# A macaron decoder trunk on one core: five instead of four down-projection units in a seven-product form, and one constant matrix instead of two

## The chip, the core and the metric

The kernel runs on one core of a Trainium2 chip. The metric is the device time of one execution in microseconds (us), as the median of several runs.

## What is computed

A trunk of two residual layers on an input of 256 tokens by 1024 features, in float32. Each layer is a feed-forward network (FFN), a token mixer, and a second FFN; a final RMSNorm follows. So there are four FFNs in the program.

```python
def swiglu(h, w_gate, w_up, w_down):
    return (jax.nn.silu(h @ w_gate) * (h @ w_up)) @ w_down
...
    for layer in range(DEPTH):
        x = x + 0.5 * swiglu(rmsnorm(x, norm_ffn1[layer]), ffn1_gate[layer], ffn1_up[layer], ffn1_down[layer])
        h = rmsnorm(x, norm_mix[layer])
        ...
        x = x + 0.5 * swiglu(rmsnorm(x, norm_ffn2[layer]), ffn2_gate[layer], ffn2_up[layer], ffn2_down[layer])
    return rmsnorm(x, norm_final)
```

What is left out between the two FFNs adds the mixer's output to `x`: stick-breaking attention with pooling in layer 0, block attention in layer 1. The hidden width of an FFN is 2816. Its down projection multiplies the hidden activations (256 tokens by 2816) by a weight matrix of 2816 by 1024.

## The kernel before

**Three passes for one product.** Every float32 operand is split into a high part (a cast to the matmul's rounded float32) and a low part (the operand minus its high part). A product takes three matmuls: high by high, high by low, low by high (`passes`, line 371). For weights, ACT makes the high part (`whi`, line 106) and DVE the low part (`wlo`, line 107), on tiles of 128 partitions by 2048 values.

**The weight stream** (`WeightStream`, lines 38 to 126) loads weights in the order of a list, 1 MB at a time, into 3 raw buffers, and splits them into 4 pairs of `whi` and `wlo` buffers. One entry of the list that is split is called a slot here. `ahead(i)` issues the splits up to three slots ahead; a slot can be split only when the matmuls of the slot four before it are done with its buffers.

**The down projection.** The 2816 hidden rows are 11 units of 256 rows (`r` from 0 to 10). A unit is computed in one of two ways:

- *plain*: 2 row tiles by 2 token halves by 2 column halves by 3 passes, 24 matmuls of 512 columns; the weights are one slot of 2048 values per partition.
- *seven* (Strassen's form): the unit is a 2 by 2 product of blocks, done with 7 block products by 3 passes, 21 matmuls of 512 columns. Its weights take two slots: the *quarters*, for which 1536 of the 2048 raw values are split, and the *sums*: `add_up` (lines 78 to 84) lets DVE make four combinations of the raw quarters with three instructions (lines 82, 83, 84) in the one buffer `sums`, which is then split like raw weights. Three of the seven products use the quarters (9 matmuls), four the sums (12 matmuls).

Below, 5q and 5s are the quarters and the sums of unit 5. `mixed` (lines 424 to 481; its matmuls are recorded at line 444) works off the units of `MIXED`: `SEVEN = [1, 3, 5, 7]`, with plain units 0, 2 and 4 between them. It uses eight PSUM banks, then recombines the products into `x` (lines 469 to 480). `rows` (lines 391 to 422; matmuls at line 413) does the units of `LAST`, all plain, the first of them as one group and the three others as a second, and adds the four accumulators to `x` (line 421).

**The hidden rows** come from the gate and up projections in chunks: chunk `c` makes units `2c-1` and `2c`, in four tiles `f` of 128 rows. `put_pairs` (line 555) follows a chunk: for a unit of the seven form, POOL makes four combinations (lines 564 to 567), ACT casts three pieces into `hs` (line 571) and DVE makes their low parts (line 572); for a plain unit ACT casts one piece into `hp` (line 575) and DVE makes its low part (line 576). In chunk 5 of the kernel before, units 9 and 10 are both plain.

**The order of the work.** Each engine runs its instructions in the order that the framework's scheduler put them in when the program was built, and waits on semaphores for the others. So an instruction that waits holds up all behind it on its engine.

**Room.** `hs` holds the seven-form hidden rows, `hp8` and `hp6` the plain ones; the mixers reuse these three buffers (`mixer_tiles`, line 603). `bcast_rstd` (line 612) turns the norm's factor of each token into a 128-partition row: a diagonal matrix (line 618) times a matrix of ones (line 619).

Of the kernel before, what the change touches and what calls it, by code (L numbers as in the profile page):

```python
# [9 lines left out]
F32 = mybir.dt.float32  # L10
F32R = mybir.dt.float32r
BF16 = mybir.dt.bfloat16
AF = mybir.ActivationFunctionType
ALU = mybir.AluOpType
PSUM = bass.MemoryType.PSUM

P = 128
T = 256
# [9 lines left out]
BIG = 1.0e37  # L28
QK_SCALE = 0.125

SEVEN = [1, 3, 5, 7]
PLAIN = [0, 2, 4, 6, 8, 9, 10]
MIXED = [1, 0, 3, 2, 5, 4, 7]
LAST = [6, 8, 9, 10]
NS = len(SEVEN)


# [114 lines left out]
def trunk_kernel(  # L152
# [6 lines left out]
    nc = tc.nc  # L159
    cp = ctx.enter_context(tc.tile_pool(name="const", bufs=1))  # L160
    wp = ctx.enter_context(tc.tile_pool(name="weights", bufs=1))
    ap_ = ctx.enter_context(tc.tile_pool(name="acts", bufs=1))
# [4 lines left out]
    def uid(s):  # L167
        cnt[0] += 1
        return f"{s}_{cnt[0]}"
# [4 lines left out]
    def tr_bank():  # L174
        return ps.tile([P, 512], F32, tag="tr", name=uid("tr"), bufs=3)

    mm = nc.tensor.matmul
# [6 lines left out]
    def add_cols(key, w, c0):  # L184
        plan[key] = [ws.add(w[0:512, c0 : c0 + 512], 4, 512), ws.add(w[512:1024, c0 : c0 + 512], 4, 512)]
# [4 lines left out]
    def add_rows(key, w, r0, seven=False):  # L190
        plan[key] = ws.add(w[r0 * P : (r0 + 2) * P, :], 2, 1024, seven)

    def add_ffn(tag, wg, wu, wd):
        add_half((tag, "g", 0), wg, 0)
        add_half((tag, "u", 0), wu, 0)
        for c in range(5):
            add_cols((tag, "g", c + 1), wg, 256 + 512 * c)
            add_cols((tag, "u", c + 1), wu, 256 + 512 * c)
        for r in MIXED + LAST:
            add_rows((tag, "d", r), wd, 2 * r, r in SEVEN)  # L200

# [52 lines left out]
    ident = cp.tile([P, P], F32, name="ident")  # L254
    make_identity(nc, ident)
    half = cp.tile([P, 1], F32, name="half")
    nc.gpsimd.memset(half, -0.5)
    ones = cp.tile([P, P], F32, name="ones")
    nc.gpsimd.memset(ones, 1.0)
    gT = [cp.tile([P, n], F32, name=f"gT{n}") for n in (16, 36)]  # L260

    def turn_gains(j):
# [24 lines left out]
    neg1 = cp.tile([P, P], F32, name="neg1")  # L287
# [195 lines left out]
    def first_products(ug, uu):  # L483

        key = ("f1", 0)
        st = states[key]
        with tc.manual_schedule():
            norm_half(0, key, st, ws.split_piece, (1,), True)
            warm_up(3)
            ws.split_to(1)  # L490
            g0 = proj(ug, 0, 256)
            ws.split_to(2)
            norm_half(1, key, st, pool_q=(0, 1))
            u0 = proj(uu, 0, 256)
            ws.split_to(4)
            g1 = proj(ug, 1, 256)
            u1 = proj(uu, 1, 256)
        return [(g0, u0), (g1, u1)]
# [14 lines left out]
    def whole(bank, t):  # L513
        nc.scalar.copy(t, bank[:, T:])  # L514
        nc.vector.tensor_add(t, t, bank[:, :T])  # L515
        return t

    def ffn(tag, st, after, then=lambda: None):
        hs = ap_.tile([P, 2, NS, 7, P], F32R, tag="hs", name=uid("hs"))
        hp = [ap_.tile([P, 2, n, T], F32R, tag=f"hp{n}", name=uid("hp")) for n in (8, 6)]  # L520
        place = {k: j for j, k in enumerate(2 * r + e for r in PLAIN for e in range(2))}

        def plain(k, n=1):

            j = place[k]
            t, j = (hp[0], j) if j < 8 else (hp[1], j - 8)
            return t[:, 0, j : j + n], t[:, 1, j : j + n]

        def put_h(m, h):
            bank = tr_bank()  # L530
            for j in range(2):
                nc.tensor.transpose(bank[:, j * P : (j + 1) * P], h[:, j * P : (j + 1) * P], ident)
            v = bank[:, :T].rearrange("p (k t) -> p k t", k=2)
            hi, lo = (t[:, :, m * P : (m + 1) * P] for t in plain(0, 2))
            nc.scalar.copy(hi, v)
            nc.vector.tensor_sub(lo, v, hi.bitcast(F32))


        ug, uu = plan[tag, "g", 0], plan[tag, "u", 0]
        banks = first_products(ug, uu) if ug[0] == 0 else None  # L540
        ws.ahead(uu[-1])
        for m in range(2):
            g, u = banks[m] if banks else (proj(ug, m, 256), proj(uu, m, 256))
            h = tp.tile([P, T], F32, tag="hw", name=uid("h"), bufs=3)
            nc.scalar.activation(h, g[:, :T], AF.Silu, scale=st[m])
            nc.vector.tensor_mul(h, u[:, :T], h)
            tasks.add(3, lambda m=m, h=h: put_h(m, h))
        box = []
        tasks.add(4, lambda: box.append(bcast_rstd(st)))
        scale = []  # L550
        for m in range(2):
            scale.append(tp.tile([P, 1], F32, tag=f"half_rstd{m}", name=uid("hr")))
            nc.gpsimd.tensor_scalar_mul(scale[m], st[m], 0.5)

        def put_pairs(h, c):

            r = [2 * c - 1, 2 * c]
            n = sum(q in SEVEN for q in r)
            if n:
                v = h.rearrange("p (j e) t -> p j e t", e=2)[:, 0:n]  # L560
                pr = slice(SEVEN.index(r[0]), SEVEN.index(r[0]) + n)
                a11, a21, row2 = v[:, :, 0, 0:P], v[:, :, 0, P:T], v[:, :, 1, :]
                s = tp.tile([P, D], F32, tag="wide", name=uid("s"), bufs=1).rearrange("p (j s t) -> p j s t", j=2, s=4)[:, 0:n]
                nc.gpsimd.tensor_add(s[:, :, 0], a21, row2[:, :, P:T])
                nc.gpsimd.tensor_sub(s[:, :, 2], a21, a11)
                nc.gpsimd.tensor_sub(s[:, :, 1], s[:, :, 0], a11)
                nc.gpsimd.tensor_sub(s[:, :, 3], row2[:, :, 0:P], s[:, :, 1])
                flat = "p j s t -> p j (s t)"
                for d, src in ((slice(0, 1), a11), (slice(1, 3), row2), (slice(3, 7), s.rearrange(flat))):
                    hi, lo = (hs[:, e, pr, d].rearrange(flat) for e in range(2))  # L570
                    nc.scalar.copy(hi, src)
                    nc.vector.tensor_sub(lo, src, hi.bitcast(F32))
            for j in range(n, 2):
                hi, lo = plain(2 * r[j], 2)
                nc.scalar.copy(hi, h[:, 2 * j : 2 * j + 2])  # L575
                nc.vector.tensor_sub(lo, h[:, 2 * j : 2 * j + 2], hi.bitcast(F32))  # L576

        for c in range(1, 6):
            ug, uu = plan[tag, "g", c], plan[tag, "u", c]
            ws.ahead(ug[-1])  # L580
            sg = tp.tile([P, 4, T], F32, tag="sg", name=uid("sg"), bufs=1)
            for f in range(5):
                if f < 4:
                    whole(proj_W(ug, f), sg[:, f])
# [12 lines left out]
        units = [(plan[tag, "d", r], 2 * r, SEVEN.index(r) if r in SEVEN else None) for r in MIXED]
        acc = mixed(units, hs, parts_of, scale)
        then()
        units = [(plan[tag, "d", r], 2 * r) for r in LAST]  # L600
        rows(acc, [units[0:1], units[1:4]], parts_of, scale, after, begun=True)

    def mixer_tiles(n_f):

        o = ap_.tile([P, 2, 8, T], F32R, tag="hp8", name=uid("o"))
        qk = ap_.tile([P, 2 * NS * 7 * P], F32, tag="hs", name=uid("qk"))
        q, k = (qk[:, j * n_f * T : (j + 1) * n_f * T].rearrange("p (f t) -> p f t", t=T) for j in range(2))
        tok = [qk[:, 4096 + j * 1024 : 5120 + j * 1024].rearrange("p (m a) -> p m a", m=2) for j in range(2)]
        room = Room(ap_.tile([P, 2 * 6 * T], F32, tag="hp6", name=uid("room")), qk[:, 6144:])
        return o[:, 0], o[:, 1], q, k, tok, room  # L610

    def bcast_rstd(st):

        bank = tr_bank()
        dg = tp.tile([P, T], F32, tag="hw", name=uid("diag"), bufs=3)
        for m in range(2):
            ms = slice(m * P, (m + 1) * P)
            nc.vector.tensor_scalar_mul(dg[:, ms], ident, st[m])
            mm(bank[:, ms], ones, dg[:, ms], start=True, stop=True)  # L619
        rb = tp.tile([P, T], F32, tag="rb", name=uid("rb"), bufs=1)  # L620
        nc.scalar.copy(rb, bank[:, :T])
        return rb
# [250 lines left out]
```

## Time and profile before

| | us |
|---|---|
| median of 3 runs | 959.95 (959.37 to 959.96) |
| the profiled execution | 959.6 |
| its span, first to last instruction | 957.8 |
| TensorE busy (matmul) | 946.8 |
| VectorE (DVE) busy | 723.3 |
| ScalarE (ACT) busy | 533.5 |
| GpSimd (POOL) busy | 84.3 |

The mean granted clock of TensorE is 0.994 of 2.4 GHz, and half of it in a stretch near the start. A matmul's duration in a row is longer than its pace, since matmuls follow each other in a pipeline: the pace is read from the starts of successive ones. On DVE and ACT too, an instruction starts about 0.1 us before the one ahead of it has ended where nothing has to be waited for.

### The profile page before, as it was taken

To read this page: it belongs to the slowest core of one execution; us is meant where nothing else is said; L and a number is where in the kernel's file an instruction comes from. 1 tells how busy PE (TensorE), PEld (TensorE's weight loads), DVE (VectorE), ACT (ScalarE), POOL (GpSimd) and SP (SyncE) were. 2 spreads that over 40 slices of the span, in tenths; PEclk is the share of its full clock that TensorE was granted. 3 is DMA by queue.
4 is the path that set the end of the run, shared out by engine and by line. 5 is a ranking of instruction groups with operands and counts; after the bars stand their busy time and mean duration, and the time that the engine had idled before them with its cause. 6 is when DMAs were issued, how large, how long until landed. Compare 5 with 4: busy or idle time off the path is not lost.

```text
span 957.8 us, 13148 instructions
## 1 busy us (share of the span) xinstructions
PE 946.8 (99%) x5236; PEld 810.4 (85%) x5236; DVE 723.3 (76%) x953; ACT 533.5 (56%) x749; POOL 84.3 (9%) x158
## 2 busy tenths in 40 slices
PE   8999999999999999999999999999999999999997
PEld 6888888888889888888898888888888798888885
DVE  5777799777656777897767779976887667778974
ACT  6566555466536665555455655536566465665541
POOL 5900000000001000000101000001000010000000
PEclk8999999999999999999999999999999999999998
DMA  7754437654335445546455543764543454445541
GB/s 276 264 177 176 176 137 259 219 177 176 93 128 176 176 176 180 216 176 215 167 208 200 178 176 133 247 233 159 178 150 122 142 177 176 177 176 179 209 161 45
DMA packets 84309, 171.53 MB, mean 179 GB/s; under 512 B 2788, under 2 KB 25880, under 8 KB 84248
## 3 DMA queue, kind: packets, MB, share of 16 engines
q1 hardware_dynamic: 83960, 170.17, 51.1%
q8 instruction: 41, 0.67, 0.3%
q10 hardware_dynamic: 288, 0.52, 0.1%
q14 instruction: 20, 0.16, 0.0%
HBM read 169.63 MB, written 1.05 MB: 178 GB/s over the span
## 4 chain that ended last, share of the span: by engine, by line
PE 98%; DMA 1%; DVE 1%; ACT 0%; issue 0%; SPq 0%; POOLq 0%; POOL 0%; ACTq 0%
PE acc L508 53%; PE acc L413 14%; PE acc L444 11%; PE acc L386 10%; PE tr L444 3%; PE tr L354 1%; PE acc L636 1%; PE tr L746 1%; PE tr L769 1%; DMA raw<-in_ffn_gate_dram 1%; PE tr L659 0%; DVE wlo L107 0%; PE tr L675 0%; PE tr L619 0%; ACT whi L106 0%; PE tr L711 0%
## 5 line engine op out<-in xcount | busy, mean ns | idle before, releaser
L107 DVE TENSOR_TENSOR wlo<-raw,whi 128x2048 fp32r<-128x2048 f32 (+3 forms) x170 | 359.5, 2120 | 98.7 <-ACT whi L106 98.0
L508 PE MATMUL acc<-xhl,whi 128*128 128x512 f32 x1472 | 372.3, 393 | 0.0
L106 ACT CAST whi<-raw 128x2048 fp32r<-128x2048 f32 (+3 forms) x170 | 299.0, 1769 | 92.0 <-PE acc L444 48.6
L508 PEld LDWEIGHTS acc<-xhl,whi 128*128 128x128 f32 x1472 | 264.7, 189 | 47.4 <-issue 0.3
L508 PEld LDWEIGHTS acc<-xhl,wlo 128*128 128x128 f32 x1472 | 200.7, 190 | 15.3 <-issue 1.3
L508 PE MATMUL acc<-xhl,wlo 128*128 128x256 f32 x1472 | 209.8, 283 | 0.0
L386 PE MATMUL acc<-whi,xhl 128*128 128x256 f32 (+1 forms) x416 | 94.3, 316 | 1.1 <-ACT whi L106 1.1
L413 PE MATMUL acc<-whi,hp 128*128 128x512 f32 x256 | 80.6, 392 | 0.0
L386 PEld LDWEIGHTS acc<-whi,xhl 128*128 128x128 f32 x416 | 70.3, 195 | 6.5 <-ACT whi L106 1.8
L386 PE MATMUL acc<-wlo,xhl 128*128 128x256 f32 (+1 forms) x208 | 65.3, 314 | 1.2 <-DVE wlo L107 1.2
L587 ACT ACTIVATE sg<-sg 128x256 f32<-128x256 f32 x80 | 33.0, 417 | 54.3 <-DVE sg L586 54.2
L444 PE MATMUL acc<-whi,hp 128*128 128x512 f32 x192 | 61.1, 389 | 0.0
L514 ACT COPY hw<-acc 128x256 f32<-128x256 f32 x104 | 38.2, 368 | 34.0 <-PE acc L508 33.9
L413 PEld LDWEIGHTS acc<-whi,hp 128*128 128x128 f32 x256 | 47.9, 188 | 9.6
L413 PE MATMUL acc<-wlo,hp 128*128 128x512 f32 x128 | 50.3, 393 | 0.0
L515 DVE TENSOR_TENSOR sg<-sg,acc 128x256 f32<-128x256 f32 x80 | 31.9, 416 | 19.2 <-ACT sg L514 19.1
L515 DVE TENSOR_TENSOR hw<-hw,acc 128x256 f32<-128x256 f32 x104 | 43.1, 414 | 4.2 <-ACT hw L514 4.0
L575 ACT CAST hp<-sg 128x512 fp32r<-128x512 f32 x24 | 14.9, 622 | 54.0 <-DVE sg L591 54.0
L514 ACT COPY sg<-acc 128x256 f32<-128x256 f32 x80 | 27.7, 367 | 31.0 <-DVE hp L576 19.0
L444 PE MATMUL acc<-whi,hs 128*128 128x512 f32 x128 | 44.6, 389 | 0.0
L413 PE MATMUL acc<-whi,o 128*128 128x512 f32 x128 | 43.6, 404 | 0.0
L386 PEld LDWEIGHTS acc<-wlo,xhl 128*128 128x128 f32 x208 | 40.6, 195 | 3.3 <-DVE wlo L107 1.6
(151 smaller groups left out, 1023.2 us busy)
## 6 DMA issues: line engine op xcount, KB each, us to landing
raw<-in_ffn_down_dram SPq DMA_DIRECT2D x44, 1024.0 KB, 4.8
raw<-in_ffn_gate_dram SPq DMA_DIRECT2D x43, 1024.0 KB, 5.0
raw<-in_ffn_up_dram SPq DMA_DIRECT2D x43, 1024.0 KB, 5.0
raw<-in_odd_w_qkv_dram SPq DMA_DIRECT2D x12, 1024.0 KB, 5.0
raw<-in_even_w_in_dram SPq DMA_DIRECT2D x8, 1024.0 KB, 5.6
raw<-in_even_w_out_dram SPq DMA_DIRECT2D x4, 1024.0 KB, 4.7
raw<-in_odd_w_o_dram SPq DMA_DIRECT2D x4, 1024.0 KB, 4.8
raw<-in_ffn_gate_dram SPq DMA_DIRECT2D x2, 512.0 KB, 6.8
```

The lines of the kernel that those rows point to most:

```text
L106: self.nc.scalar.copy(hi[:, d], src)
L107: self.nc.vector.tensor_sub(lo[:, d], src, hi[:, d].bitcast(F32))
L354: nc.tensor.transpose(bank[:, j * P : (j + 1) * P], x[m][:, k * P : (k + 1) * P], ident)
L386: mm(bank[:, :width], a, b, start=(n == 0), stop=(n == len(seq) - 1))
L413: mm(acc[m, n], a, b, start=(done[m, n] == 0 and p == 0 and not begun), stop=(done[m, n] == total - 1 and p == 2), skip_group_check=begun)
L444: mm(b, l, r, start=b.name not in begun, stop=last and n == 2, skip_group_check=True)
L508: mm(dst, w, rhs, start=(n == 0), stop=(n == 2 * KD - 1))
L514: nc.scalar.copy(t, bank[:, T:])
L515: nc.vector.tensor_add(t, t, bank[:, :T])
L575: nc.scalar.copy(hi, h[:, 2 * j : 2 * j + 2])
L587: nc.scalar.activation(sg[:, f - 1], sg[:, f - 1], AF.Silu)
L636: mm(bank[j * HD : (j + 1) * HD, cols], v[:, 0 if start else 1, hs], a[:, s], start=start, stop=not start)
```

## The change

Unit 9 joins the seven form. `MIXED` loses the plain unit 4 and gets unit 9 at its end, so that units 5, 7 and 9 stand in a row, without a plain unit between them; unit 4 becomes the first of `LAST`, before 6, 8 and 10. `hs` grows by a quarter, `hp6` becomes `hp4`, and the mixers' room moves accordingly. The matrix of ones goes: the diagonal is multiplied by -1 in the same instruction, and the matrix of minus ones, which the program has anyway, takes the place of the ones.

```diff
--- before.py
+++ after.py
@@ -28,10 +28,10 @@
 BIG = 1.0e37
 QK_SCALE = 0.125
 
-SEVEN = [1, 3, 5, 7]
-PLAIN = [0, 2, 4, 6, 8, 9, 10]
-MIXED = [1, 0, 3, 2, 5, 4, 7]
-LAST = [6, 8, 9, 10]
+SEVEN = [1, 3, 5, 7, 9]
+PLAIN = [0, 2, 4, 6, 8, 10]
+MIXED = [1, 0, 3, 2, 5, 7, 9]
+LAST = [4, 6, 8, 10]
 NS = len(SEVEN)
 
 
@@ -255,8 +255,6 @@
     make_identity(nc, ident)
     half = cp.tile([P, 1], F32, name="half")
     nc.gpsimd.memset(half, -0.5)
-    ones = cp.tile([P, P], F32, name="ones")
-    nc.gpsimd.memset(ones, 1.0)
     gT = [cp.tile([P, n], F32, name=f"gT{n}") for n in (16, 36)]
 
     def turn_gains(j):
@@ -517,7 +515,7 @@
 
     def ffn(tag, st, after, then=lambda: None):
         hs = ap_.tile([P, 2, NS, 7, P], F32R, tag="hs", name=uid("hs"))
-        hp = [ap_.tile([P, 2, n, T], F32R, tag=f"hp{n}", name=uid("hp")) for n in (8, 6)]
+        hp = [ap_.tile([P, 2, n, T], F32R, tag=f"hp{n}", name=uid("hp")) for n in (8, 4)]
         place = {k: j for j, k in enumerate(2 * r + e for r in PLAIN for e in range(2))}
 
         def plain(k, n=1):
@@ -606,7 +604,7 @@
         qk = ap_.tile([P, 2 * NS * 7 * P], F32, tag="hs", name=uid("qk"))
         q, k = (qk[:, j * n_f * T : (j + 1) * n_f * T].rearrange("p (f t) -> p f t", t=T) for j in range(2))
         tok = [qk[:, 4096 + j * 1024 : 5120 + j * 1024].rearrange("p (m a) -> p m a", m=2) for j in range(2)]
-        room = Room(ap_.tile([P, 2 * 6 * T], F32, tag="hp6", name=uid("room")), qk[:, 6144:])
+        room = Room(ap_.tile([P, 2 * 4 * T], F32, tag="hp4", name=uid("room")), qk[:, 6144:])
         return o[:, 0], o[:, 1], q, k, tok, room
 
     def bcast_rstd(st):
@@ -615,8 +613,8 @@
         dg = tp.tile([P, T], F32, tag="hw", name=uid("diag"), bufs=3)
         for m in range(2):
             ms = slice(m * P, (m + 1) * P)
-            nc.vector.tensor_scalar_mul(dg[:, ms], ident, st[m])
-            mm(bank[:, ms], ones, dg[:, ms], start=True, stop=True)
+            nc.vector.tensor_scalar(dg[:, ms], ident, st[m], -1.0, op0=ALU.mult, op1=ALU.mult)
+            mm(bank[:, ms], neg1, dg[:, ms], start=True, stop=True)
         rb = tp.tile([P, T], F32, tag="rb", name=uid("rb"), bufs=1)
         nc.scalar.copy(rb, bank[:, :T])
         return rb
```

The lines behind the two that go have a number lower by 2 in the changed kernel, so line 444 is 442 there, and 413 is 411.

**DVE, down projection of an FFN** (here the first; the others are alike). `wlo<-sums` is the low part of a sums slot, `wlo<-raw` of 1536 values that of a quarters slot, of 2048 values that of a plain unit; the first row is 5s. Before:

```order
L107 TENSOR_TENSOR wlo_1532<-sums_1533,whi_1531 128x2048
L82 TENSOR_TENSOR sums_1598<-raw_1504 128x1024
L107 TENSOR_TENSOR wlo_1566<-raw_1474,whi_1565 128x2048
L83 TENSOR_TENSOR sums_1598<-raw_1504,sums_1598 128x512
L84 TENSOR_TENSOR sums_1598<-raw_1504,sums_1598 128x512
L107 TENSOR_TENSOR wlo_1581<-raw_1504,whi_1580 128x1536
L107 TENSOR_TENSOR wlo_1597<-sums_1598,whi_1596 128x2048
```

The changed kernel, from the same instruction (5s):

```order
L107 TENSOR_TENSOR wlo_1539<-sums_1540,whi_1538 128x2048
L107 TENSOR_TENSOR wlo_1573<-raw_1481,whi_1572 128x1536
L82 TENSOR_TENSOR sums_1587<-raw_1481 128x1024
L83 TENSOR_TENSOR sums_1587<-raw_1481,sums_1587 128x512
L84 TENSOR_TENSOR sums_1587<-raw_1481,sums_1587 128x512
L107 TENSOR_TENSOR wlo_1586<-sums_1587,whi_1585 128x2048
L107 TENSOR_TENSOR wlo_1608<-raw_1511,whi_1607 128x1536
L82 TENSOR_TENSOR sums_1622<-raw_1511 128x1024
L83 TENSOR_TENSOR sums_1622<-raw_1511,sums_1622 128x512
L84 TENSOR_TENSOR sums_1622<-raw_1511,sums_1622 128x512
L107 TENSOR_TENSOR wlo_1621<-sums_1622,whi_1620 128x2048
L107 TENSOR_TENSOR wlo_1643<-raw_1546,whi_1642 128x2048
```

Before, the sums of unit 7 (lines 82 to 84) stand around the low part of plain unit 4 (`wlo_1566`), ahead of 7q and 7s. Now the low part of 7q follows 5s at once, then come the three instructions for the sums of 7, 7s, and the same again for 9; unit 4 (`wlo_1643`) comes after 9s.

**ACT, chunk 5 of the gate and up stage.** `hw` is the copy of an up tile, `hp` and `hs` the casts of hidden rows, `whi` the high part of weights; the last row of both pieces is the cast for plain unit 0. Before:

```order
L514 COPY hw_1377<-acc_1360 128x256
L575 CAST hp_134<-sg_1240 128x512
L514 COPY hw_1398<-acc_1381 128x256
L106 CAST whi_1435<-raw_1236 128x2048
L514 COPY hw_1419<-acc_1402 128x256
```

The changed kernel:

```order
L512 COPY hw_1375<-acc_1358 128x256
L569 CAST hs_130<-sg_1238 128x128
L569 CAST hs_130<-sg_1238 128x256
L569 CAST hs_130<-s_1421 128x512
L512 COPY hw_1396<-acc_1379 128x256
L106 CAST whi_1442<-raw_1234 128x2048
L512 COPY hw_1417<-acc_1400 128x256
```

Where one cast of unit 9 into `hp` stood, three into `hs` stand now, the last of them from POOL's combinations `s`; the copies of the next up tile and the weight cast are behind it.

**PE, the end of the last seven-form unit.** `acc` and `tr` are PSUM banks. Before, from the last product of 7s (`whi_1596`, `wlo_1597`) into plain unit 6 (`whi_1630`):

```order
L444 MATMUL acc_1429<-whi_1596,hs_132 128x512
L444 MATMUL acc_1429<-wlo_1597,hs_132 128x512
L444 MATMUL acc_1429<-whi_1596,hs_132 128x512
L413 MATMUL acc_1428<-whi_1630,hp_133 128x512
L413 MATMUL acc_1428<-wlo_1631,hp_133 128x512
L413 MATMUL acc_1428<-whi_1630,hp_133 128x512 x2
```

The changed kernel, from the last matmul of 9q (`whi_1607`) into 9s (`whi_1620`, `wlo_1621`) and unit 4 (`whi_1642`):

```order
L442 MATMUL acc_1435<-whi_1607,hs_130 128x512
L442 MATMUL acc_1438<-whi_1620,hs_130 128x512
L442 MATMUL tr_1441<-whi_1620,hs_130 128x512
L442 MATMUL tr_1440<-whi_1620,hs_130 128x512
L442 MATMUL acc_1436<-whi_1620,hs_130 128x512
L411 MATMUL acc_1435<-whi_1642,hp_131 128x512
L411 MATMUL acc_1434<-whi_1642,hp_131 128x512
L411 MATMUL acc_1437<-whi_1642,hp_131 128x512
L442 MATMUL acc_1438<-wlo_1621,hs_130 128x512
L442 MATMUL acc_1438<-whi_1620,hs_130 128x512
L442 MATMUL tr_1441<-wlo_1621,hs_130 128x512
```

Before, each product has its three passes in a row. Now four high-by-high matmuls of 9s come first, then three matmuls of unit 4 that need its high part alone, and then those of 9s that need the low part.

## Rows read from the trace of the kernel before

**Rows 1.** The page, busy time of each engine (share of the span, number of instructions).

```profile
PE 946.8 (99%) x5236; PEld 810.4 (85%) x5236; DVE 723.3 (76%) x953; ACT 533.5 (56%) x749; POOL 84.3 (9%) x158
```

**Rows 2.** The page, the chain of work that ended last, share of the span by engine.

```profile
PE 98%; DMA 1%; DVE 1%; ACT 0%; issue 0%; SPq 0%; POOLq 0%; POOL 0%; ACTq 0%
```

**Rows 3.** TensorE in the second FFN's down projection: the first matmul of line 444 in the timeline (start us, duration us, engine, line, operation), then pieces of the chain of waits in order of time (start us, length us, engine, tile and line, number of matmuls).

```profile
411.78 0.40 PE L444 MATMUL tr<-whi,hs 128*128 128x512 f32 x1
...
411.95 0.70 PE tr L444 x3
...
416.05 6.12 PE acc L444 x27
...
447.33 0.68 PE acc L413 x3
```

**Rows 4.** The timeline of DVE, end of the second FFN's gate and up stage and its down projection (start us, duration us, engine, line, operation, out<-in with shapes, count, idle time before and its releaser).

```profile
408.30 0.41 DVE L591 TENSOR_TENSOR sg<-hw,sg 128x256 f32<-128x256 f32 x1
...
412.06 2.29 DVE L107 TENSOR_TENSOR wlo<-raw,whi 128x2048 fp32r<-128x2048 f32 x1 [1.17 <-ACT whi L106]
...
414.60 1.75 DVE L107 TENSOR_TENSOR wlo<-raw,whi 128x1536 fp32r<-128x1536 f32 x1
416.27 0.42 DVE L591 TENSOR_TENSOR sg<-hw,sg 128x256 f32<-128x256 f32 x1
...
419.41 2.28 DVE L107 TENSOR_TENSOR wlo<-raw,whi 128x2048 fp32r<-128x2048 f32 x1
421.61 1.22 DVE L82 TENSOR_TENSOR sums<-raw 128x1024 f32<-128x1024 f32 x1
...
423.59 0.69 DVE L84 TENSOR_TENSOR sums<-raw,sums 128x512 f32<-128x512 f32 x1
424.20 1.75 DVE L107 TENSOR_TENSOR wlo<-raw,whi 128x1536 fp32r<-128x1536 f32 x1
426.34 2.29 DVE L107 TENSOR_TENSOR wlo<-sums,whi 128x2048 fp32r<-128x2048 f32 x1 [0.39 <-ACT whi L106]
...
446.80 0.68 DVE L470 TENSOR_TENSOR p1u<-p1u,tr 128x512 f32<-128x512 f32 x1
447.40 0.74 DVE L476 SCALAR_TENSOR_TENSOR x<-p1u,hr,x 128x512 f32<-128x512 f32 x1
448.06 0.68 DVE L471 TENSOR_TENSOR u<-p1u,acc 128x512 f32<-128x512 f32 x1
```

**Rows 5.** The timeline of ACT, same stretch and just behind it, same columns.

```profile
410.12 1.91 ACT L106 CAST whi<-raw 128x2048 fp32r<-128x2048 f32 x1 [0.48 <-PE acc L508]
...
424.39 1.92 ACT L106 CAST whi<-sums 128x2048 fp32r<-128x2048 f32 x1 [0.66 <-DVE sums L84]
...
467.68 5.53 ACT L106 CAST whi<-raw 128x2048 fp32r<-128x2048 f32 x3 [3.58 <-issue]
```

**Rows 6.** Timelines of DVE, ACT and POOL where the second FFN splits the hidden rows of unit 7 (chunk 4): DVE's low part of 128 values and the product that completes the unit, ACT's last cast for it and the weight cast behind it, POOL's last addition for it.

```profile
385.40 0.39 DVE L572 TENSOR_TENSOR hs<-sg,hs 128x128 fp32r<-128x128 f32 x1
385.72 0.41 DVE L591 TENSOR_TENSOR sg<-hw,sg 128x256 f32<-128x256 f32 x1
...
387.92 0.62 ACT L571 CAST hs<-s 128x512 fp32r<-128x512 f32 x1 [1.35 <-POOL s L567]
...
388.71 1.92 ACT L106 CAST whi<-raw 128x2048 fp32r<-128x2048 f32 x1
...
387.43 0.46 POOL L567 TENSOR_TENSOR s<-sg,s 128x128 f32<-128x128 f32 x1
```

**Rows 7.** Timelines of POOL and DVE near the program's start, where POOL makes the pooling bands: two subtractions of line 321 at one time and two at another, and DVE's instructions beside them.

```profile
36.31 0.88 POOL L321 TENSOR_TENSOR band<-band,ident 128x128 f32<-128x128 f32 x2
...
38.69 5.03 POOL L321 TENSOR_TENSOR band<-band,ident 128x128 f32<-128x128 f32 x2
...
37.04 0.44 DVE L586 TENSOR_TENSOR sg<-sg,rb 128x256 f32<-128x256 f32 x1
38.57 2.29 DVE L107 TENSOR_TENSOR wlo<-raw,whi 128x2048 fp32r<-128x2048 f32 x1 [1.10 <-ACT whi L106]
40.78 0.41 DVE L515 TENSOR_TENSOR sg<-sg,acc 128x256 f32<-128x256 f32 x1
41.11 2.28 DVE L107 TENSOR_TENSOR wlo<-raw,whi 128x2048 fp32r<-128x2048 f32 x1
43.32 0.68 DVE L586 TENSOR_TENSOR sg<-sg,rb 128x256 f32<-128x256 f32 x1
```

**Rows 8.** The page, DMA issues: the loads of down-projection weights (queue, number, KB each, us from issue to landing).

```profile
raw<-in_ffn_down_dram SPq DMA_DIRECT2D x44, 1024.0 KB, 4.8
```

**Rows 9.** Who waited for whom, of the weight loads: us in total, times, longest us.

```profile
PEld acc L413 <- DVE wlo L107: 1.1, 4, 0.3
```

**Rows 10.** Busy time in four stretches near the start (us from the span's start: length, busy us and instructions of PE, PEld, DVE, ACT, POOL; then TensorE's granted clock as a share of 2.4 GHz, DMA share, GB/s).

```profile
7.00:11.00 4.00, 1.87 (x9) 0.95 (x7) 3.22 (x4) 2.96 (x7) 1.72 (x2) 0.94 1.08 381
11.00:16.00 5.00, 4.81 (x22) 4.81 (x23) 3.75 (x7) 2.54 (x5) 1.86 (x3) 0.50 1.06 390
16.00:20.00 4.00, 4.00 (x31) 4.00 (x30) 1.38 (x2) 2.89 (x5) 2.50 (x2) 0.83 1.01 384
33.00:34.00 1.00, 0.75 (x5) 0.35 (x3) 1.00 (x4) 0.00 (x0) 1.00 (x3) 1.00 0.61 131
```

**Rows 11.** Who waited for whom, of the matmuls: us in total, times, longest us.

```profile
PE tr L619 <- DVE diag L618: 0.3, 1, 0.3
```

## The prediction

> **What bounds the kernel now.** The page's busy times come first: TensorE is busy for 946.8 of the 957.8 us span, DVE for 723.3 [rows 1]. The chain of waits puts 98% of the span on TensorE [rows 2]. So a matmul that goes is time won, as long as TensorE still finds its operands ready; the question is whether DVE and ACT, which prepare them, keep up where the change loads them more. That is read in the down projection. There, TensorE runs without a gap: 27 matmuls take 6.12 us, 0.2267 us each, and the 156 from 411.95 to 447.33 us keep that pace [rows 3]. All times below count from its first matmul at 411.78 us, called t0 [rows 3], in the second FFN; the three others are alike.
>
> **What is removed.** Unit 9 takes 21 matmuls in place of 24, in four FFNs: 12 x 0.2267 = 2.7 us less. Unit 4 only moves.
>
> **What is added, and where it lies.** DVE gets per FFN three instructions of sums (421.61 to 424.28, 2.7 us) and low parts of 1.75 + 2.28 in place of one of 2.29 us [rows 4]; ACT gets a longer split too. None of this is on the path by its amount alone. It gets there by order, in four steps.
>
> *1. Chunk 5.* Before, the product that completes unit 9's hidden rows ends at 408.71 [rows 4], and ACT casts the weights of unit 0 from 410.12 on [rows 5]; DVE starts their low part at 412.06, t0 + 0.28 [rows 4]. Now ACT has three casts to make, the last after POOL's additions, with the weight cast behind it in its queue. Chunk 4 shows the price: the product ends at 386.13 and the weight cast starts at 388.71, 2.58 us later [rows 6]. That gives 408.71 + 2.58 = 411.29, so 1.17 us later than 410.12.
>
> *2. POOL beside DVE.* In chunk 5, unlike chunk 4, DVE has two sums instructions (lines 83 and 84) among these rows. What that does is seen near the start: two subtractions on POOL that took 0.88 us at 36.31 took 5.03 at 38.69, beside two DVE subtractions of 2.29 and 2.28; the second ended at 43.72, 0.33 after DVE's did at 43.39; and DVE's next one took 0.68 where 0.44 is usual [rows 7]. Each engine holds up the other. So an addition on POOL ends 0.33 after the DVE instruction in its way, and a DVE instruction in POOL's way ends 0.28 after it (44.00 against 43.72), its own duration less 0.16. Applied to chunk 5: from the end of the unit's product, DVE's line 570 on 128 values (0.39 long where chunk 4 has it [rows 6], begun just before) lasts about 0.3, POOL's second addition until 0.62, DVE's line 84 until 1.17, POOL's third until 1.50, DVE's line 570 on 256 until 1.78, POOL's last until 2.11; in chunk 4 the last ends after 1.76, at 387.89 [rows 6]. That is 0.35 more; and the product itself is pushed by some 0.15, since POOL's first addition meets line 83. Together 0.5 us. The bounds are 0 (POOL always finds DVE between two such instructions) and about 1.0 (each of three additions waits for a DVE instruction of some 0.7 us, half of it new). I take 0.5, as worked out. So unit 0's low part starts at t0 + 0.28 + 1.17 + 0.5 = t0 + 1.95. The Trainium skill, page "SBUF — State Buffer", section "Who interferes with whom", states that VectorE and GpSimd share a pair of ports under an exclusive lock. By that rule the 0.5 us belong in the sum, and the 5.03 us agree; without it the time would be that of the first rival.
>
> *3. Up to 5s.* From unit 0's low part to that of 5s DVE's order is unchanged, and it takes 426.34 - 412.06 = 14.28 us; the one idle piece that the rows have there, 0.39, is the wait for the cast of the sums, which moves along [rows 4]. Nothing absorbs the delay: 5s starts at t0 + 16.23.
>
> *4. From 5s to 9s.* Before, a plain unit's split lay between two sets of sums, so that ACT's cast of the sums ran beside other work of DVE. Now it is a single file, by the order and the one `sums` buffer: low part of 5s 2.20 (419.41 to 421.61, an equal one), of 7q 1.67 (414.60 to 416.27), sums of 7 2.67 (421.61 to 424.28) [rows 4], 0.11 until ACT's cast at 424.39, which takes 1.92 [rows 5], 0.03 until DVE's low part of 7s at 426.34. That is 8.60 us per unit, and TensorE uses up a seven-form unit in 21 x 0.2267 = 4.76. Twice 8.60: DVE's low part of 9s starts at t0 + 33.43, and its cast is done at t0 + 33.40.
>
> **The waits.** Ahead of 9s TensorE has 5 x 9 + 4 x 12 + 2 x 24 = 141 matmuls and gets there at t0 + 31.96. It waits 1.44 us for the cast of 9s. It runs four matmuls (0.91), to t0 + 34.31, and then needs the cast of unit 4. That is behind 9s in ACT's queue, whose successive casts come 1.84 us apart (5.53 for three) [rows 5]: t0 + 35.24, a wait of 0.93. The three matmuls of unit 4 and the low part of 9s, ready at 35.7, follow closely. In sum 2.37 us per FFN, 9.5 us in four.
>
> **Covered.** Later low parts just come in time: eviction instructions of 0.60 to 0.67 us [rows 4] stand between them on DVE; unit 8 is ready near t0 + 44.2 and unit 10 near t0 + 49.0, and TensorE's new order asks for them 0.3 us later each. If that cover is gone, it is the third rival. Weight loads land 4.8 us after issue [rows 8]; unit 9's buffer comes free with unit 2's split, near t0 + 12, and 9q is cast after t0 + 22. The present waits of weight loads for low parts in `rows`, 1.1 us in four [rows 9], lie in the order that is gone; about half of them, 0.4 us, I count as TensorE time won (bounds 0 and 1.1). The matrix of minus ones and the second multiplication cost nothing: the low end is 0, the high end a wait as long as the one for the diagonal, 0.3 us [rows 11]. The moved rooms of the mixers are free long before their use, since the rows that held them are read last in the FFN before, as they were.
>
> **Sum.** -2.7 - 0.4 + 9.5 = +6.4 us. Against the profiled execution's own 959.6: 966.0. The median of the runs is 959.95, 0.35 above it, so I predict 966.3 us, 0.66% slower. A measurement of this kernel can tell about 0.2%, 1.9 us, from no change.
>
> **The rivals.**
>
> - *POOL and DVE don't meet in chunk 5.* Step 2 falls away, the waits are 0.94 + 0.93 = 1.87, four of them 7.5, and the time 964.3. For it: in chunk 4 POOL's additions pass without much delay. Against it: the two DVE instructions that now stand there. 0.20.
> - *No difference.* ACT is not held up in chunk 5 at all, and the low part of unit 0 stays at t0 + 0.28. Then the cast of 9s is ready at 31.73, before TensorE asks, and that of unit 4 at 33.57, 0.70 after it asks: 4 x 0.7 - 3.1 = -0.3, 959.7 us. Against it: ACT keeps its order, and chunk 4 shows the wait. 0.10.
> - *Later low parts come late too.* Should units 8 and 10 lose their 0.3 us, some 0.5 us each per FFN comes on top: 970.3. 0.06.
> - *Faster.* The file of step 4 ends before TensorE needs it: the point is the cast of unit 4 at t0 + 32.87, 2.4 us earlier than I work out. Then only the gain is left, 959.95 - 3.1 = 956.8. Against it: each of its pieces is a row that occurs in this trace many times with the same length. 0.06.
> - *The clock falls.* Between 7 and 11 us TensorE was busy for 1.87 of 4 us, and the granted clock, at 2.4 GHz before, was 0.50 of it from 11 to 16 and 0.83 in the mean to 20 [rows 10]: some 6.8 us at 1.2 GHz, a loss of 3.4. Here two waits with 0.91 us of work between them make a stretch of 3.3 us. If it does the same in every FFN, the time is 966.3 + 13.7 = 980.0. Against it: full activity on both sides, and a gap at 33 us that left the clock at 1.00 [rows 10]. The Trainium skill, "TensorE: Matmul & The Clock Gate", section "HAM oscillation — how this bites in real kernels", describes kernels that lose the full clock again after each wait; the trace bears that out at the start alone. 0.06.
>
> **Numbers.** My forecast has 0.52. Its own uncertainty, step 2 between 0 and 1.0 us and the 0.4, gives 964 to 969. The range from 962.0 to 969.5 takes in the first rival and the lower part of the third. Faster 0.06, same 0.10, slower 0.84.
>
> **What would show it.** Right: in each FFN two waits of TensorE, 0.5 to 2 us for the cast (line 106) of 9s at line 442 and some 0.9 us at line 411; low parts of 5s, 7s and 9s 8.6 us apart; unit 0's low part near t0 + 2; 12 fewer matmuls. Wrong: TensorE without gaps at lines 442 and 411, low parts closer than 8 us, or a granted clock of 0.5 behind the waits.

## The result, and the profile after

The changed kernel takes 966.34 us (median of four runs, 964.16 to 968.03), the kernel before 959.85 beside it: a ratio of 1.0074, 95% interval 1.0060 to 1.0087. That is 0.7% slower, with 12 matmuls fewer. The execution profiled took 968.03 us (span 966.3).

Busy times of the engines and the chain of waits of the changed kernel, from the page:

```profile
PE 946.6 (98%) x5224; PEld 808.5 (84%) x5224; DVE 744.8 (77%) x977; ACT 540.0 (56%) x761; POOL 88.6 (9%) x173
...
PE 52%; DVE 23%; ACT 10%; issue 9%; POOL 3%; DMA 1%; SPq 0%; ACTq 0%; POOLq 0%; DVEq 0%
```

Read the two lines against [rows 1, 2]. The busy time of TensorE hardly moves. The chain does: TensorE had 98% of it and has 52%, and DVE, ACT and POOL stand in it where they did not. So something now reaches back from a late matmul through ACT to DVE and POOL. The chain's share of these engines is not time lost: TensorE is busy beside nearly all of it. Who waited for whom says where (us in total, times, longest us; of the matmuls):

```profile
PE acc L442 <- ACT whi L106: 5.0, 4, 1.3
PE acc L411 <- ACT whi L106: 2.4, 4, 0.6
```

Both waits come four times, once in each FFN, and the waits of weight loads for low parts [rows 9] are gone. What a wait costs is read from the starts of the matmuls in TensorE's timeline, second FFN (start us, us, line, count, idle time before):

```profile
445.65 0.39 PE L442 MATMUL acc<-whi,hs 128*128 128x512 f32 x1
447.33 0.50 PE L442 MATMUL acc<-whi,hs 128*128 128x512 f32 x1 [1.29 <-ACT whi L106]
447.67 0.62 PE L442 MATMUL tr<-whi,hs 128*128 128x512 f32 x2
448.13 0.40 PE L442 MATMUL acc<-whi,hs 128*128 128x512 f32 x1
449.14 1.54 PE L411 MATMUL acc<-whi,hp 128*128 128x512 f32 x3 [0.61 <-ACT whi L106]
450.48 0.63 PE L442 MATMUL acc<-wlo,hs 128*128 128x512 f32 x1
450.91 0.63 PE L442 MATMUL acc<-whi,hs 128*128 128x512 f32 x1
...
452.88 0.39 PE L442 MATMUL acc<-wlo,hs 128*128 128x512 f32 x1
```

From 445.65 to 447.33 are 1.68 us where 0.23 is the pace: 1.45 lost. From 448.13 to 449.14 are 1.01: 0.78 lost. Behind the second wait the starts come 0.43 apart, nearly twice the pace, until 452.88: the clock, below.

Back along the chain. DVE's timeline from chunk 5 on (answers to [rows 4]; t0, the first matmul of line 442, is 413.90 here), then POOL's and ACT's of the same stretch:

```profile
409.82 0.90 DVE L83 TENSOR_TENSOR sums<-raw,sums 128x512 f32<-128x512 f32 x1
410.65 0.41 DVE L589 TENSOR_TENSOR sg<-hw,sg 128x256 f32<-128x256 f32 x1
...
411.19 0.96 DVE L84 TENSOR_TENSOR sums<-raw,sums 128x512 f32<-128x512 f32 x1
412.07 0.68 DVE L570 TENSOR_TENSOR hs<-sg,hs 128x256 fp32r<-128x256 f32 x1
...
415.84 2.29 DVE L107 TENSOR_TENSOR wlo<-raw,whi 128x2048 fp32r<-128x2048 f32 x1 [0.60 <-ACT whi L106]
...
430.12 2.29 DVE L107 TENSOR_TENSOR wlo<-sums,whi 128x2048 fp32r<-128x2048 f32 x1 [0.39 <-ACT whi L106]
432.33 1.75 DVE L107 TENSOR_TENSOR wlo<-raw,whi 128x1536 fp32r<-128x1536 f32 x1
434.00 1.22 DVE L82 TENSOR_TENSOR sums<-raw 128x1024 f32<-128x1024 f32 x1
...
438.72 2.29 DVE L107 TENSOR_TENSOR wlo<-sums,whi 128x2048 fp32r<-128x2048 f32 x1 [2.05 <-ACT whi L106]
...
447.31 2.29 DVE L107 TENSOR_TENSOR wlo<-sums,whi 128x2048 fp32r<-128x2048 f32 x1 [2.04 <-ACT whi L106]
```

```profile
411.14 0.46 POOL L562 TENSOR_TENSOR s<-sg 128x128 f32<-128x128 f32 x1 [0.96 <-DVE sg L589]
411.68 0.79 POOL L564 TENSOR_TENSOR s<-s,sg 128x128 f32<-128x128 f32 x1
412.55 0.52 POOL L565 TENSOR_TENSOR s<-sg,s 128x128 f32<-128x128 f32 x1
```

```profile
413.10 0.62 ACT L569 CAST hs<-s 128x512 fp32r<-128x512 f32 x1 [1.60 <-POOL s L565]
...
413.89 1.91 ACT L106 CAST whi<-raw 128x2048 fp32r<-128x2048 f32 x1
...
445.38 1.90 ACT L106 CAST whi<-sums 128x2048 fp32r<-128x2048 f32 x1 [5.32 <-DVE sums L84]
447.19 3.70 ACT L106 CAST whi<-raw 128x2048 fp32r<-128x2048 f32 x2
```

Unit 0's weight cast starts behind POOL's last addition, at t0 - 0.01 instead of t0 - 1.66 [rows 3, 5]; its low part at t0 + 1.94 instead of t0 + 0.28. The low parts of 5s, 7s and 9s stand 8.60 and 8.59 us apart, DVE idle for 2.05 in each file, while ACT casts the sums. And the cast of 9s ends at 447.28, 0.05 before the late matmul.

The granted clock, in stretches behind the waits of the second FFN and, in the last row, of the third (columns as in [rows 10]):

```profile
448.00:450.00 2.00, 1.39 (x5) 0.82 (x4) 2.00 (x2) 2.00 (x2) 0.00 (x0) 0.82 0.84 340
450.00:452.00 2.00, 2.00 (x6) 1.55 (x5) 2.00 (x2) 2.00 (x3) 0.00 (x0) 0.50 0.00 0
452.00:454.00 2.00, 2.00 (x8) 1.59 (x8) 2.00 (x2) 1.18 (x1) 0.00 (x0) 0.83 0.52 92
...
637.00:641.00 4.00, 4.00 (x19) 3.23 (x18) 4.00 (x3) 2.85 (x3) 0.00 (x0) 1.00 0.29 91
```

At 2.4 GHz until the waits, TensorE ran at 1.2 GHz for some 3.4 us behind them in the second FFN; what the three rows lack to a clock of 1.00, (0.18 + 0.50 + 0.17) x 2.00 = 1.7 us, is lost. In the other three FFNs, with waits of 1.28 to 1.47 and 0.77 to 0.78 us, the clock stayed at 1.00.

### The profile page after: what moved, and what is told of

The parts are those of the page before. It is cut to its first block, busy times and chain, and to the rows that moved or that the text cites. A ratio compares the mean times of both kernels' runs of the same rounds, so it can differ in the third digit from the quotient of the medians.

```text
span 966.3 us, 13183 instructions
## 1 busy us (share of the span) xinstructions
PE 946.6 (98%) x5224; PEld 808.5 (84%) x5224; DVE 744.8 (77%) x977; ACT 540.0 (56%) x761; POOL 88.6 (9%) x173
## 4 chain that ended last, share of the span: by engine, by line
PE 52%; DVE 23%; ACT 10%; issue 9%; POOL 3%; DMA 1%; SPq 0%; ACTq 0%; POOLq 0%; DVEq 0%
PE acc L506 21%; PE acc L411 14%; DVE wlo L107 11%; PE acc L384 9%; ACT whi L106 7%; PE acc L442 2%; DVE sums L82 2%; DVE sg L589 2%; DVE hw L513 2%; DVE sg L513 2%; DVE sums L83 1%; PE acc L634 1%; PE tr L352 1%; POOL s L564 1%; DVE hp L574 1%
## 5 line engine op out<-in xcount | busy, mean ns | idle before, releaser
L411 PE MATMUL acc<-whi,hp 128*128 128x512 f32 x256 | 81.0, 395 | 2.4 <-ACT whi L106 2.4
L106 ACT CAST whi<-sums 128x2048 fp32r<-128x2048 f32 x20 | 38.3, 1913 | 51.6 <-DVE sums L84 46.3
L442 PE MATMUL acc<-whi,hs 128*128 128x512 f32 x160 | 57.1, 394 | 5.0 <-ACT whi L106 5.0
L107 DVE TENSOR_TENSOR wlo<-sums,whi 128x2048 fp32r<-128x2048 f32 x20 | 45.8, 2289 | 18.0 <-ACT whi L106 18.0
L563 POOL TENSOR_TENSOR s<-sg 128x128 f32<-128x128 f32 x20 | 9.2, 461 | 393.6 <-DVE sg L589 393.6
L442 PE MATMUL tr<-whi,hs 128*128 128x512 f32 x120 | 43.8, 392 | 0.0
```

Source lines behind the costliest of these rows:

```text
L106: self.nc.scalar.copy(hi[:, d], src)
L107: self.nc.vector.tensor_sub(lo[:, d], src, hi[:, d].bitcast(F32))
L411: mm(acc[m, n], a, b, start=(done[m, n] == 0 and p == 0 and not begun), stop=(done[m, n] == total - 1 and p == 2), skip_group_check=begun)
L442: mm(b, l, r, start=b.name not in begun, stop=last and n == 2, skip_group_check=True)
```

## The experiments

A run moves by up to 3.5 us with the start of the program, where TensorE has the same instructions in every kernel here: the first down projection begins between 136.4 and 139.9 us, as the clock stands low for more or less of the time up to 20 us. So beside each time there is a length that the start doesn't touch: from the first matmul of the first FFN's down projection to the end of the span, cut at the first matmul of each further down projection (from TensorE's timeline, one profiled execution each; the span is taken to 0.1 us).

| kernel | FFN 1 to 2 | 2 to 3 | 3 to 4 | 4 to end | sum | against before |
|---|---|---|---|---|---|---|
| before | 272.58 | 183.56 | 297.84 | 64.62 | 818.60 | |
| changed | 273.97 | 186.66 | 299.44 | 66.30 | 826.37 | +7.77 |
| changed_again | 274.01 | 186.52 | 299.32 | 66.34 | 826.19 | +7.59 |
| minus_ones_alone | 272.59 | 183.53 | 297.82 | 64.58 | 818.52 | -0.08 |
| chunk5_as_before | 272.43 | 183.38 | 297.79 | 64.67 | 818.27 | -0.33 |
| no_late_sums | 273.34 | 184.42 | 298.65 | 65.62 | 822.03 | +3.43 |
| two_in_a_row | 272.56 | 183.47 | 297.87 | 64.63 | 818.53 | -0.07 |
| sums_first | 272.35 | 183.54 | 297.80 | 64.73 | 818.42 | -0.18 |
| apart | 276.05 | 186.73 | 299.70 | 66.00 | 828.48 | +9.88 |
| one_apart | 272.10 | 183.06 | 297.49 | 63.81 | 816.46 | -2.14 |
| one_apart_sums_first | 271.76 | 182.54 | 296.99 | 63.73 | 815.02 | -3.58 |
| four_sums_first | 272.54 | 183.59 | 297.86 | 64.56 | 818.55 | -0.05 |

Of one program's variants that differ in nothing that TensorE waits for (before, minus_ones_alone, two_in_a_row, four_sums_first) the sums agree within 0.1 us, far closer than the times do. Edits are against the changed kernel unless said; ratios are to the kernel before on the same chip.

**changed_again**: no edit. 

> The changed kernel once more. My theory: waits of 1.45 and 0.8 us in each FFN, 966.3 us. What is open is the clock: behind the two waits of the second FFN it stood at 0.66 for some 4 us in the execution profiled, in the three others at 1.00. If it falls in some FFNs of some executions, the runs spread from 963.5 to 968.5, and the stretch of this profile that falls need not be the second; if it belongs to the second FFN it falls there again and nowhere else.

Measured: 966.01 us, ratio 1.0074 (1.0053 to 1.0094), the same two waits of 5.0 and 2.5 us in four. The clock falls behind the second FFN's waits again and nowhere else between start and end:

```profile
448.00:450.00 2.00, 2.00 (x5) 1.61 (x6) 2.00 (x2) 2.00 (x2) 0.00 (x0) 0.50 0.15 61
450.00:452.00 2.00, 2.00 (x8) 1.57 (x7) 2.00 (x2) 1.98 (x2) 0.00 (x0) 0.72 0.36 29
```

So it fell in the second FFN in two executions of two, though not at the same place: at t0 + 35.4 in the first, just behind the second wait, and at t0 + 35.0 in this one, within it. Why there, I can't say; two executions don't show that it belongs to this FFN, and the six others have no trace.

**minus_ones_alone**: the kernel before, with this part only:

```diff
-            nc.vector.tensor_scalar_mul(dg[:, ms], ident, st[m])
-            mm(bank[:, ms], ones, dg[:, ms], start=True, stop=True)
+            nc.vector.tensor_scalar(dg[:, ms], ident, st[m], -1.0, op0=ALU.mult, op1=ALU.mult)
+            mm(bank[:, ms], neg1, dg[:, ms], start=True, stop=True)
```

> The kernel before with one part of the change alone: the matrix of ones dropped for that of minus ones, with the second multiplication by -1. My theory: nothing, 957 to 959.5 us, the kernel before's own time, and all of the 0.74% belongs to the fifth unit. Rival: the longer DVE instruction keeps a waiting TensorE longer, 0.3 us in each of six broadcasts, 0.2% above.

Measured: 957.27 against 958.68, ratio 0.9987 (0.9975 to 0.9998); in the table -0.08 us. The lengths behind the start don't show the difference in time. This part costs nothing.

**chunk5_as_before**:

```diff
-            n = sum(q in SEVEN for q in r)
+            n = sum(q in SEVEN for q in r) if c < 5 else 0
...
-                hi, lo = plain(2 * r[j], 2)
+                hi, lo = (hs[:, e, 4, 0:4].rearrange("p (k a) t -> p k (a t)", k=2) for e in range(2)) if r[j] == 9 else plain(2 * r[j], 2)
...
-        units = [(plan[tag, "d", r], 2 * r, SEVEN.index(r) if r in SEVEN else None) for r in MIXED]
+        units = [(plan[tag, "d", r], 2 * r, min(SEVEN.index(r), 3) if r in SEVEN else None) for r in MIXED]
```

> The fifth seven-form unit stays, but its hidden rows are written in chunk 5 as a plain unit's (one cast, no additions on POOL); its products read the hidden rows of unit 7. Left out: the combinations of unit 9's hidden rows. My theory (the late start in chunk 5 uses up the slack, the single file of 8.6 us per unit turns it into waits): DVE's low part of unit 0 is back near t0 + 0.3, TensorE has no wait for the cast of 9s at line 442 and some 0.7 us for that of unit 4 at line 411, so 959.7 us, between 958.5 and 961. Rival A, the single file alone makes the waits, whatever chunk 5 does: two waits of some 2.4 us in each FFN stay and the time is 966. Rival B, something else in the changed program is slow (the matrix of minus ones, the moved rooms): 966 without waits at these lines.

Measured: 958.32 us, ratio 1.0000 (0.9990 to 1.0011); -0.33 in the table. The wait at line 442 is gone, that at 411 is 0.5 us. DVE's low parts of units 0, 7s and 9s (t0 is 410.26), and the one wait left:

```profile
410.53 2.29 DVE L107 TENSOR_TENSOR wlo<-raw,whi 128x2048 fp32r<-128x2048 f32 x1 [1.14 <-ACT whi L106]
...
433.41 2.29 DVE L107 TENSOR_TENSOR wlo<-sums,whi 128x2048 fp32r<-128x2048 f32 x1 [2.05 <-ACT whi L106]
...
442.01 2.29 DVE L107 TENSOR_TENSOR wlo<-sums,whi 128x2048 fp32r<-128x2048 f32 x1 [2.05 <-ACT whi L106]
```

```profile
PE acc L411 <- ACT whi L106: 2.0, 4, 0.5
```

The single file is untouched, 8.60 us per unit, and yet nearly all of the loss goes: with unit 0's low part at t0 + 0.27 the file ends 0.2 us before TensorE asks for 9s. With the start on time the file costs 0.7 us per FFN more than the kernel before loses there, about what the fifth unit gains; the rest of the loss takes the late start as well.

**no_late_sums**:

```diff
+        if self.sevens.index(r) % 5 == 1: return
         self.nc.vector.tensor_sub(t[:, 2], b[:, 2], t[:, 0])
         self.nc.vector.tensor_sub(t[:, 3], b[:, 3], t[:, 2])
...
+            if self.sevens.index(r) % 5 == 1: src = src[:, None, 0:1024].to_broadcast([P, 2, 1024])
```

> Only lines 83 and 84 of one unit go: the two later sums of unit 3, which DVE makes in chunk 5 beside POOL's additions. Left out: that half of unit 3's sums; its first half is cast and split twice instead, so that every later instruction stays. My theory (step 2: POOL and DVE hold each other up by 0.5 us and this lies on the path): POOL's third addition takes 0.60 us instead of 0.79, unit 0's low part starts at t0 + 1.45 instead of 1.94, the wait for 9s falls from 1.45 to some 0.95 us, and the time is 964.3. Rival, the hold lies beside other work and ACT alone sets the start: t0 + 1.9 and 966.3 as the changed kernel. Should DVE's load in chunk 5 be the bound, the start comes earlier than t0 + 1.2 and the time is below 963.5.

Measured: 962.05 us, ratio 1.0042 (1.0031 to 1.0052). POOL's last two additions for unit 9 and DVE's product that completes the unit and its low part of unit 0 (t0 is 411.71), then TensorE's waits (the line numbers are 4 higher here):

```profile
409.10 0.60 POOL L568 TENSOR_TENSOR s<-s,sg 128x128 f32<-128x128 f32 x1
409.77 0.46 POOL L569 TENSOR_TENSOR s<-sg,s 128x128 f32<-128x128 f32 x1
...
408.07 0.41 DVE L593 TENSOR_TENSOR sg<-hw,sg 128x256 f32<-128x256 f32 x1
...
413.00 2.29 DVE L111 TENSOR_TENSOR wlo<-raw,whi 128x2048 fp32r<-128x2048 f32 x1 [0.60 <-ACT whi L110]
```

```profile
PE acc L415 <- ACT whi L110: 2.4, 4, 0.6
PE acc L446 <- ACT whi L110: 2.4, 4, 0.7
```

Without DVE's two sums in its way POOL's additions take their usual 0.60 and 0.46 us, and the start comes at t0 + 1.29, 0.65 earlier. The wait for 9s falls from 5.0 to 2.4 us in four, 0.65 each. Not all of the 0.65 is step 2, since DVE's own work on line 83 goes too: the product ends at t0 - 3.23, 0.16 earlier than in the kernel before (t0 - 3.07), which has that line and no additions on POOL. That leaves 0.49. So POOL and DVE do hold each other up, on the path. The total moves by more, 4.3 us in the table: three FFNs give 0.63 to 0.79, the second 2.24. The difference of some 1.5 us is the clock, which stays at 1.00 here from 444 to 452 us.

**two_in_a_row**: the kernel before, four seven-form units, with another order:

```diff
-MIXED = [1, 0, 3, 2, 5, 4, 7]
-LAST = [6, 8, 9, 10]
+MIXED = [1, 0, 3, 2, 5, 7]
+LAST = [4, 6, 8, 9, 10]
...
-        rows(acc, [units[0:1], units[1:4]], parts_of, scale, after, begun=True)
+        rows(acc, [units[0:2], units[2:5]], parts_of, scale, after, begun=True)
```

> The kernel before, with four seven-form units, but unit 4 behind unit 7, so that 5 and 7 stand in a row without a plain unit between. My theory: one file of 8.6 us starts on time; the cast of 7s is ready near t0 + 23.1 and TensorE asks for it at t0 + 27.2, so no wait, 959.9 us (959 to 961). Rival A, sevens in a row cost 2.4 us per FFN by themselves: 969.

Measured: 958.06 us, ratio 0.9997 (0.9986 to 1.0009), no wait in the down projection. DVE's low part of 7s comes at t0 + 23.2 (t0 is 408.93), as worked out:

```profile
432.14 2.29 DVE L107 TENSOR_TENSOR wlo<-sums,whi 128x2048 fp32r<-128x2048 f32 x1 [2.05 <-ACT whi L106]
```

Two seven-form units in a row cost nothing when the start is on time; three are not tried here.

**sums_first**:

```diff
-            if part == "sums":
+            if part == "quarters":
                 self.add_up(r)
...
-        self.nc.vector.tensor_sub(lo[:, d], src, hi[:, d].bitcast(F32))
+        with self.tc.issue_after(self.summed) if part == "quarters" else nullcontext():
+            self.nc.vector.tensor_sub(lo[:, d], src, hi[:, d].bitcast(F32))
```

> The changed kernel; DVE's low part of a unit's quarters is put behind that unit's sums, so that ACT casts the sums while DVE makes that low part. My theory (the single file of 8.6 us has some 2.05 us of DVE idle per unit, and it alone makes the waits): low parts of 5s, 7s and 9s stand some 6.6 us apart, the waits at lines 442 and 411 shrink to below 0.5 us in each FFN, and the time is some 6 us below the changed kernel's, 1 to 3 us above the kernel before on the same chip. Rival: another thing holds the file (the load of the weights, ACT's own load): low parts stay 8 us or more apart and the time stays 0.7% above the kernel before.

Measured: 958.15 us against 958.48, ratio 0.9998 (0.9988 to 1.0008). DVE in the file of 9s:

```profile
435.31 2.29 DVE L108 TENSOR_TENSOR wlo<-sums,whi 128x2048 fp32r<-128x2048 f32 x1 [0.40 <-ACT whi L106]
437.64 1.22 DVE L82 TENSOR_TENSOR sums<-raw 128x1024 f32<-128x1024 f32 x1
...
440.24 1.75 DVE L108 TENSOR_TENSOR wlo<-raw,whi 128x1536 fp32r<-128x1536 f32 x1
442.38 2.29 DVE L108 TENSOR_TENSOR wlo<-sums,whi 128x2048 fp32r<-128x2048 f32 x1 [0.39 <-ACT whi L106]
```

The idle time falls from 2.05 to 0.39 us, the file from 8.60 to 7.07 (I had 6.6), and the loss goes; a gain does not come, since the low part of 9s is now what a matmul waits for (443.79 to 444.72, 0.70 lost). Either end of the cause, the late start or the idle time in the file, removed by itself takes the loss away; neither by itself leaves the gain.

**apart**:

```diff
-MIXED = [1, 0, 3, 2, 5, 7, 9]
-LAST = [4, 6, 8, 10]
+MIXED = [1, 0, 3, 2, 5, 4, 7, 6, 9]
+LAST = [8, 10]
```

> The changed kernel with its five seven-form units apart: 1, 0, 3, 2, 5, 4, 7, 6, 9, then 8 and 10. My theory: a plain unit's split lies between any two sets of sums, so no wait at lines 442 and 411, and 2.7 us less work than before. But the results of the seven-form units (eight instructions of 0.6 to 0.7 us on DVE) and two low parts of 2.3 us now fall into the last two units' 10.9 us of TensorE, so that the new bound is there: waits of the next stage's first instructions (lines 352 and 384) of some 1.6 us in an FFN. In sum 4 to 6 us above the kernel before with these waits, 3 us below it without.

Measured: 969.75 us, ratio 1.0106 (1.0091 to 1.0120): slower than the changed kernel, and outside what I expected. The waits at lines 442 and 411 are gone, and these stand in their place, three FFNs each (columns as above); below them the clock behind the second FFN:

```profile
PE tr L352 <- DVE x L419: 2.2, 3, 0.7
PE acc L384 <- ACT xhl L358: 2.2, 3, 0.7
PE acc L384 <- DVE xhl L359: 2.1, 3, 0.7
```

```profile
476.00:478.00 2.00, 1.30 (x10) 1.10 (x9) 2.00 (x4) 1.26 (x3) 0.58 (x2) 0.92 0.25 33
478.00:480.00 2.00, 2.00 (x11) 2.00 (x11) 2.00 (x3) 1.22 (x2) 0.64 (x2) 0.50 0.96 330
480.00:482.00 2.00, 2.00 (x15) 2.00 (x15) 2.00 (x3) 0.35 (x1) 0.00 (x0) 0.73 0.42 162
```

The place was right, the size not. There are three waits instead of one, since the late results hold up the transposes, then both halves of the next stage; and behind them TensorE falls to 1.2 GHz in the first two FFNs (0.50 from 202 to 204 us as well), 1.7 us each by the same working as above.

**one_apart**:

```diff
-MIXED = [1, 0, 3, 2, 5, 7, 9]
-LAST = [4, 6, 8, 10]
+MIXED = [1, 0, 3, 2, 5, 4, 7, 9]
+LAST = [6, 8, 10]
```

> The changed kernel with unit 4 between 5 and 7: 1, 0, 3, 2, 5, 4, 7, 9, then 6, 8 and 10. My theory: only 9 stands in a row, its file starts 2 us earlier in TensorE's time, no wait at lines 442 and 411, and with three units at the end the results of the seven-form units nearly have room (a wait of 0.5 us at line 352). In sum 1 us above to 2 us below the kernel before. Rival, any two sevens in a row at the end cost the 2.4 us per FFN: 0.7% above.

Measured: 956.23 us, ratio 0.9977 (0.9967 to 0.9988). No wait at lines 442 and 411; of the end only this is left:

```profile
PE tr L352 <- DVE x L419: 0.6, 2, 0.3
```

One plain unit ahead of 7 gives TensorE 5.4 us more work before it asks for 9s, and three units at the end nearly cover the results. The 2.1 us in the table are at the edge of what I expected.

**one_apart_sums_first**: both edits. 

> Both at once: unit 4 between 5 and 7, and each unit's sums ahead of its quarters' low part on DVE. My theory: no waits of TensorE are left in the down projections, and of the 12 matmuls 1 to 3 us remain as gain: 0.1% to 0.3% below the kernel before.

Measured: 956.11 us, ratio 0.9962 (0.9946 to 0.9979), -3.58 in the table, without a wait of TensorE in or behind the down projections. This version beats both kernels. In the table it gains a little more than the 1 to 3 us that I expected.

**four_sums_first**: the kernel before with the edit of sums_first. 

> The kernel before, with four seven-form units, and the same reordering alone: each unit's sums ahead of its quarters' low part on DVE. My theory: the kernel before has no wait that this could take away beyond the 1.1 us of weight loads on low parts, so it stays within 1 us of it; what the version with the fifth unit, unit 4 between and sums first gains (0.4%) is the fifth unit's. Rival: the reordering gains by itself, in places that I have not looked at, and this kernel too comes out 0.3% to 0.4% faster.

Measured: 959.36 against 958.68, ratio 1.0003 (0.9988 to 1.0018), -0.05 in the table. The reordering gains nothing by itself; the 3.58 us are the fifth unit's.

## Why the prediction was right

*The gain* of 2.7 us is there: one_apart_sums_first, without waits, gains 3.58, which is 0.9 more than the matmuls. The waits of weight loads in `rows` are 0.6 of this, where I took 0.4 (its bounds were 0 and 1.1). In the kernel before they show at one place of each FFN, here in the second:

```profile
455.79 0.50 PE L413 MATMUL acc<-wlo,hp 128*128 128x512 f32 x1
456.12 0.63 PE L413 MATMUL acc<-whi,hp 128*128 128x512 f32 x2
```

These starts are 0.33 us apart, 0.11 more than the pace; with the matmuls around them it is 0.15 us per FFN. The other 0.3 us lie behind the down projections, and I had not counted them.

*Steps 1 and 2, chunk 5.* Unit 0's low part at t0 + 1.94 against t0 + 1.95 forecast. The instructions end as worked out: counted from the end of the product (411.06), POOL's last addition ends at 2.01 where I had 2.11. chunk5_as_before undoes both steps and the loss goes; no_late_sums undoes step 2, and with it 0.16 us of DVE's own work, which leaves 0.49 us of its 0.65 where I had 0.5, and so decides against the rival in which POOL and DVE don't meet. The Trainium skill, page "SBUF — State Buffer", section "Who interferes with whom", speaks of an exclusive lock between VectorE and GpSimd; POOL's 0.79 us beside DVE and 0.60 without agree with it.

*Steps 3 and 4, the file.* 5s at t0 + 16.22 (16.23 forecast), units 8.60 apart, 9s at t0 + 33.41 (33.43). two_in_a_row shows that one pair without a late start does no harm, chunk5_as_before that three in a row need the late start for most of theirs, sums_first that the idle 2.05 us within the file are the other half.

*The waits* cost 1.45 and 0.78 us in the second FFN where I had 1.44 and 0.93; 1.28 and 0.77 in the first, 1.47 and 0.78, 1.46 and 0.77 in the others: 8.8 in all. The first matmuls behind each wait start 0.1 us further apart than the pace (447.33 to 447.67), which I had not counted: 0.9 more. Together 9.7 against 9.5.

*The sum.* 9.7 - 2.7 - 0.6 = 6.4 us, and with the clock's 1.7 us 8.1, against 7.77 in the table; the 0.3 between them are gained behind the down projections of the first three FFNs. So the +6.4 holds for what it described, within 0.3 (7.77 less 1.7 is 6.1), while the clock adds what I had given a chance of 0.06 and for all four FFNs at once. That rival is true in one FFN of four, and a granted clock of 0.5 behind the waits was one of my signs of being wrong. The Trainium skill, "TensorE: Matmul & The Clock Gate", section "HAM oscillation — how this bites in real kernels", tells of a kernel that loses the full clock at every wait for a load, waits that are longer than the two here; the trace bears that out in the second FFN alone, where the waits are those of the third to 0.02 us. That the median, 966.34, falls on 966.3 has luck in it: the start moves each run by more than these remainders, and hid most of the clock's 1.7 us. Run again beside the kernel before (changed_again), the two medians are 8.1 us apart, 966.01 and 957.89.

*Later low parts*, the third rival: no wait for units 6, 8 or 10 stands among TensorE's waits. *The matrix of minus ones* costs nothing.

## What to carry to other kernels

A producer line (here ACT and DVE, 8.6 us per unit) that takes longer per unit than its consumer (TensorE, 4.76) is harmless as long as its head start covers the units that stand in a row, so work out the head start and the deficit per unit together, and look for what the change does to the start. Where an engine idles within the file because its next operand is being made by another, two instructions that don't depend on each other can be exchanged. Here that took the loss away (-0.18 in the table), one plain unit between did more (-2.14), and the two together most (-3.58). And before moving work behind a wait to the end of a stage, see what already waits there: apart cured one wait and made three.

## What was not expected of the hardware

Two waits of 1.45 and 0.78 us with 0.9 us of work between were followed by some 3.4 us at 1.2 GHz in the second FFN, in both executions profiled, and not in the three others; waits of 0.6 to 0.7 us in the same place (no_late_sums) left the clock at 2.4 GHz, and three of 0.7 us in apart lowered it in the first two FFNs and not in the third. What sets the second FFN apart stays open, and whether it is the FFN at all or the moment at which its waits come. A matmul that starts behind a wait is followed by its neighbour after 0.34 us instead of 0.23; the same step, 0.31 to 0.34 us, stands in the kernel before where TensorE goes between the transposes of line 354 and the matmuls of line 413 without idle time.
